# Two transformer blocks on one core: three edits to the order of work in the mixer, and SBUF pools moved to one address rest

## The chip, the cores and the metric

The kernel runs on one core of a Trainium2 chip. Its time is the device time of that core in microseconds (us). Five engines work side by side, each through its own queue in order: PE multiplies matrices, with its weight loads shown apart as PEld; DVE does vector arithmetic; ACT does copies, casts and functions such as exp and sigmoid; POOL helps with a few additions; SP issues the DMA transfers. Instructions wait for each other through semaphores. A transfer brings data from the main memory (DRAM) to SBUF, the on-chip memory, which has 128 partitions; PE writes its sums to PSUM banks, which DVE and ACT read.

## The reference, cut to what matters

The sequence has 512 positions and a width of 1024. The first block has two layers (attention over chunks, then attention through a low-rank latent, each with a convolutional feed-forward part); its result goes to the second block, a feed-forward part, a mixer and another feed-forward part:

```python
x = first_block(x, ...)           # 2 layers: attention + conv FFN each
h = h + 0.5 * gt1 * swiglu(u, w1_gate, w1_up, w1_down)
proj = modulate(rmsnorm(h)) @ w_in          # qa, ka, va, xm, o_pre, ga, gb
ya = diff_attention(qa, ka, va, lam, g_subln)   # 8 heads, p0 - lam * p1, rmsnorm per head
yb = mlstm_branch(xm, o_pre, ...)               # 4 heads of 256 rows, chunkwise mLSTM
merged = sigmoid(ga) * (ya @ w_proj_a) + sigmoid(gb) * (yb @ w_proj_b)
h = h + gt2 * (merged @ w_out)
h = h + 0.5 * gt3 * swiglu(u, w2_gate, w2_up, w2_down)
```

All of it is float32.

## The kernel before, in words

Activations lie transposed, 1024 rows as eight tiles of 128 x 512. A float32 operand is split into two parts of lower precision: the high part by a cast on ACT (`uh`, `yh`, `hidh`, `wh`), the low part as the difference on DVE (`ul`, `hidl`, `wl`). A product of a 128 x 128 weight block and a 128 x 512 tile is then three matmuls (`mm3`, lines 328 to 330: high by high, high by low, low by high). `gemm` runs these over the blocks of one output tile: 24 matmuls for eight blocks. `wload` (L305) fetches a weight row of 1024 columns into one of four `wr` buffers by a DMA on SP's queue and splits it, in one of three `wh` and three `wl` buffers.

Each feed-forward part makes 22 hidden tiles (`hid`, split in two), in groups of eight, eight and six. It multiplies every group by its rows of the down projection. The last three hidden tiles of a part go through `tail` (L431), where `tail_weights` (L421) has split the rest of the weights into four `tw` tiles: the columns are done in two halves of 256, so that the next norm's sum of squares (`colsum`, L365, with `L368` as its matmul) and its normalised tiles of the first half are made while PE works on the second. The output projection of the attentions and of the mixer has the same form, five blocks as full products and three in `tail`.

The mixer (`mix`, L994) does the differential attention (`diff`), then the mLSTM, then the output projection. At the end of the differential attention stand the gate products (`wga`, their sums in the `ps_g` banks, of which there are three) and the projections `wpa` of the attention's result. At L1354 two gate products are written ahead of the loop over the eight output tiles; each turn of the loop takes the sigmoid of the oldest gate sum, makes one `wpa` product, and one further gate product.

`ml_heads` (L1150) runs over the four mLSTM heads. Each makes two tiles `y` (`normed`, L1220). Those of heads 0 to 2 are stored to DRAM (L1245) and fetched again after the heads (L1265), since nothing in SBUF held them; those of head 3 are used in place. `gate` (L1249) makes the gate products `wgb` between the heads' steps. Then come the `wpb` products in groups of three, three and two, the first six blocks of a group ahead of its last two (L1269). Only then does `mix` open the pool `pt`, load the tail weights `woutt` and do the output projection.

The code gives the dependences; the layer that builds the program puts each engine's instructions in an order of its own, so matmuls of several products lie between each other. The order shown below is that of the built programs. Pools are laid out in SBUF by the size of what they hold. The address of a tile within its partition, taken mod 512 bytes ("rest"), is 192 for the split activations `uh`, `ul` and for the split weights `wh`, `wl` in the pool `gp`. The pool `pf` of the first feed-forward part has its hidden tiles `hidh`, `hidl` and its `tw` at rest 192, those of the three later ones have them at rest 128. In the mLSTM's pool `pl` most tiles are at rest 384.

Of the kernel before, what the change touches and what calls it, by code (L numbers as in the profile page):

```python
# [11 lines left out]
F32 = mybir.dt.float32  # L12
F32R = mybir.dt.float32r
I32 = mybir.dt.int32
AF = mybir.ActivationFunctionType
ALU = mybir.AluOpType
PSUM = bass.MemoryType.PSUM

T = 512
P = 128  # L20
# [264 lines left out]
class _K:  # L285
# [186 lines left out]
    def softmax(self, pool, s, n, add, scale, pn):  # L472

        nc = self.nc
        st = self.gp.tile([P, 4], F32, tag="st", bufs=12, name="st")
        p = pool.tile([P, T], F32, tag="p", bufs=pn, name="p")
        nc.vector.tensor_tensor_reduce(p[:, :n], s[:, :n], add, -scale, BIG, ALU.add, ALU.min, accum_out=st[:, 0:1])  # L477
        nc.scalar.activation(p[:, :n], p[:, :n], AF.Exp, bias=st[:, 0:1], scale=-1.0, accum_out=st[:, 1:2])  # L478
        nc.vector.reciprocal(st[:, 2:3], st[:, 1:2])
        return p, st  # L480
# [363 lines left out]
    def rope_tables(self, pr):  # L844
        nc, a = self.nc, self.a

        hpi = pr.tile([P, 1], F32, tag="hpi", name="hpi")
        nc.gpsimd.memset(hpi, math.pi / 2)
        sgn = pr.tile([P, 1], F32, tag="sgn", name="sgn")
        nc.gpsimd.memset(sgn, 1.0)  # L850
        for g in range(4):
            nc.gpsimd.affine_select(sgn[32 * g:32 * g + 32], sgn[32 * g:32 * g + 32], pattern=[[0, 1]],
                                    compare_op=ALU.is_ge, fill=-1.0, base=-16, channel_multiplier=1)
        self.cos = pr.tile([P, T], F32, tag="cos", name="cos")
        self.sin = pr.tile([P, T], F32, tag="sin", name="sin")

        def fill():
            pi32 = self.tmp(dt=I32, tag="acc", bufs=3)
            nc.sync.dma_start(pi32, a["pos"].to_broadcast([P, T]))
            ang = self.tmp(tag="acc", bufs=3)  # L860
            nc.vector.tensor_copy(ang, pi32)
# [12 lines left out]
            nc.scalar.activation(n, ang, AF.Abs)  # L874
            nc.scalar.activation(self.cos, n, AF.Sin, bias=hpi, scale=-1.0)
            nc.scalar.activation(self.sin, ang, AF.Sin)
            nc.vector.tensor_scalar(self.sin, self.sin, sgn, None, ALU.mult)

        return fill
# [114 lines left out]
    def mix(self, norm, ada):  # L994
        nc, a, gp = self.nc, self.a, self.gp
        u = norm.u
        with self.tc.tile_pool(name="px", bufs=1) as px:
            mg = self.diff(u, px)
            self.mlstm(u, mg)
            with self.tc.tile_pool(name="pt", bufs=1) as pt:  # L1000
                tw = self.tail_weights(pt, [("tw", 4)] * 4, "woutt")
                mm = [self.hl(gp, "u", 16, mg[k]) for k in range(8)]
                gt = ada(5)
                for j in range(8):
                    w = self.wload(a["wout"][j], HEAD * P)
                    self.resid(j, self.gemm(w, mm[:HEAD]), gt[:, j:j + 1])
                norm = self.norm_of("g_ff2", ada(7), ada(6))
                self.tail(tw, mm[HEAD:], gt, norm)
        self.dump("hx", self.h)
        return norm  # L1010

    def mlstm(self, u, mg):
        nc, a, gp = self.nc, self.a, self.gp
        dram = {n: [self.dp.tile([P, T], F32, tag=f"{n}{j}", name=f"{n}{j}") for j in range(8)]
                for n in ("mv", "xc", "xs", "so", "sg", "y")}
        for n in ("mq", "mk"):
            dram[n] = [self.dp.tile([4, P, T], F32, tag=f"{n}{h}", name=f"{n}{h}") for h in range(4)]
        with self.tc.tile_pool(name="pl", bufs=1) as pl:
            plc = pl.tile([4, 7 * P], F32, tag="plc", name="plc")
            nc.sync.dma_start(plc, a["pl"])  # L1020
            tri = pl.tile([P, P], F32, tag="tri", name="tri")
            nc.sync.dma_start(tri, a["tri"])
            slr = [pl.tile([P, T], F32, tag="slr", bufs=2, name="slr") for _ in range(2)]
            for q in range(2):
                nc.sync.dma_start(slr[q], a["slr"][q])
            brow = pl.tile([4, T], F32, tag="brow", name="brow")
            self.ml_prep(pl, u, dram, plc, slr, brow)
            self.ml_heads(pl, u, mg, dram, plc, tri, slr, brow)

    def ml_prep(self, pp, u, dram, plc, slr, b):  # L1030
        nc, a = self.nc, self.a
# [2 lines left out]
        nc.gpsimd.memset(wr[:, :960], 0.0)  # L1034
        nc.sync.dma_start(wif32[:, :, 0:8], a["wif"])
        nc.sync.dma_start(wif32[:, :, 32:40], a["wif"])
        wif = pp.tile([P, 24, 40], F32R, tag="wifr", name="wifr")
        nc.scalar.copy(wif, wif32)
        nc.vector.tensor_tensor(wif[:, :, 32:40], wif32[:, :, 32:40], wif[:, :, 0:8].bitcast(F32), ALU.subtract)
        big = lambda: pp.tile([P, T], F32, tag="stg", bufs=5, name="stg")  # L1040
# [109 lines left out]
    def ml_heads(self, pl, u, mg, dram, plc, tri, slr, b):  # L1150
        nc, a, gp = self.nc, self.a, self.gp

        def back(n, j):
            t = pl.tile([P, T], F32, tag="stg", bufs=5, name=n)
            nc.sync.dma_start(t, dram[n][j])
            return t
# [60 lines left out]
                    nc.tensor.matmul(den[:, P * j:], self.onesr, sw[j][q], start=j + q == 0, stop=j + q == 4)  # L1217
            return num, den

        def normed(h, num, den):  # L1220


            em = self.pg()
# [13 lines left out]
            for e in range(2):  # L1237
                j = 2 * h + e
                so, xs = back("so", j), back("xs", j)
                t = self.tmp(tag="tn", bufs=2)  # L1240
                nc.vector.scalar_tensor_tensor(t, num[e], self.col("g_mlnorm", j), r, ALU.mult, ALU.mult)
                nc.vector.tensor_tensor(t, t, so, ALU.mult)
                nc.vector.tensor_tensor(t, t, xs, ALU.add)
                if h < 3:
                    nc.sync.dma_start(dram["y"][j], t)  # L1245
                y.append(t)
            return y
# [4 lines left out]
            nc.scalar.copy(t, self.gemm(w, u))  # L1252
            nc.sync.dma_start(dram["sg"][j], t)

        sw, vt = scores(0), values(0)
        for h in range(4):
            gate(2 * h)
            nxt = scores(h + 1) if h < 3 else None
            gate(2 * h + 1)
            o = output(h, sw, vt)  # L1260
            if h < 3:
                vt = values(h + 1)
            y = normed(h, *o)
            sw = nxt
        ybs = [self.hl(gp, "u", 16, back("y", j)) for j in range(6)] + [self.hl(gp, "u", 16, t) for t in y]  # L1265
        for js in ((0, 1, 2), (3, 4, 5), (6, 7)):
            ws = [self.wload(a["wpb"][j]) for j in js]
            pss = [self.pg() for _ in js]
# [5 lines left out]
            for j, ps in zip(js, pss):  # L1274
                t = back("sg", j)
                nc.scalar.activation(t, t, AF.Sigmoid)
                nc.vector.tensor_tensor(t, ps, t, ALU.mult)
                nc.vector.tensor_tensor(mg[j], mg[j], t, ALU.add)

    def diff(self, u, px):  # L1280
        nc, a, gp = self.nc, self.a, self.gp
# [2 lines left out]
        with self.tc.tile_pool(name="pd", bufs=1) as pd:  # L1284
# [4 lines left out]
            lv = pd.tile([P, 4, 64], F32, tag="lv", name="lv")  # L1289
            for j in range(4):  # L1290
                nc.sync.dma_start(lv[:, j], a["lam"][j:j + 1, :].to_broadcast([P, 64]))
            lc = pd.tile([P, 4], F32, tag="lc", name="lc")
            for j in range(2):
                nc.vector.tensor_tensor_reduce(lv[:, 2 * j], lv[:, 2 * j], lv[:, 2 * j + 1], 1.0, 0.0, ALU.mult,
                                               ALU.add, accum_out=lc[:, j:j + 1])
# [1 line left out]

            nc.vector.tensor_tensor(lc[:, 2:3], lc[:, 1:2], lc[:, 0:1], ALU.subtract)
            nc.vector.tensor_scalar(lc[:, 2:3], lc[:, 2:3], -0.2, None, ALU.add)
            gsub = pd.tile([P, 1], F32, tag="gsub", name="gsub")  # L1300
            nc.vector.tensor_scalar(gsub, self.col("g_subln"), 0.8, None, ALU.mult)
            v32s = {}

# [47 lines left out]
                return probs, v, P, done  # L1351

            self.heads(pd, 8, begin)
            ga = [self.gemm(self.wload(a["wga"][j]), u) for j in range(2)]  # L1354
            slots = [("qk", 10)] * 6 + [("vs", 4)] * 4 + [("p", 4)] * 4 + [("qk", 10)] * 2
            yas = []
            for j, y in enumerate(y32):
                h, l = [pd.tile([P, T], F32R, tag=t, bufs=n, name="yh") for t, n in slots[2 * j:2 * j + 2]]
                self.split(y, h, l)
                yas.append((h, l))  # L1360
            mg = []
            for j in range(8):
                t = self.tmp(tag="acc", bufs=3)
                nc.scalar.activation(t, ga.pop(0), AF.Sigmoid)
                m = px.tile([P, T], F32, tag="mg", bufs=8, name="mg")
                nc.vector.tensor_tensor(m, self.gemm(self.wload(a["wpa"][j]), yas), t, ALU.mult)
                mg.append(m)
                if j < 6:
                    ga.append(self.gemm(self.wload(a["wga"][j + 2]), u))
        return mg  # L1370


# [21 lines left out]
```

## Time and profile before

| | us |
|---|---|
| median of three runs | 2698.45 (2692.15 to 2702.66) |
| the profiled execution | 2697.24 |
| its span, first to last instruction | 2695.5 |
| PE busy | 2587.6 |
| DVE busy | 1756.0 |
| ACT busy | 1204.9 |

The span begins with the first instruction and ends with the last, so the profiled execution has 1.7 us around it. Positions below are us from the span's start. PE is the engine that has work in 96% of the span. A matmul's own duration overlaps the next one's, so for a train of matmuls the distance from one start to the next tells the rate, and the duration does not. The granted clock of PE is given as a share of full speed: 1.00 is 2.4 GHz and 0.50 is 1.2 GHz.

### The profile page before, as it was taken

The page shows a single profiled execution, that of the slowest core. Times are in us where ns is not written, and L with a number is a line of the kernel's source. Part 1 is how long each engine was busy: PE and PEld are TensorE (multiplying, and loading weights), DVE is VectorE, ACT ScalarE, POOL GpSimd, SP SyncE. Part 2 cuts the span into 40 slices and gives each one's busy share as a digit, 9 for nine tenths or more (in the row PEclk, how much of TensorE's full clock was granted, in tenths as well). Part 3 has the DMA queues.
Part 4 walks back from the last instruction along what each step waited for, and adds up shares of the span by engine and source line. Part 5 has one row for each costly group of instructions (what it writes and reads, how often), then busy time and mean ns, then how long its engine had stood idle before and what let it go on. Part 6 is the DMA issues. An engine that isn't in the chain of part 4 may idle for free. (4 is left out here: it accounts for less than half of the span.)

```text
span 2695.5 us, 34803 instructions
## 1 busy us (share of the span) xinstructions
PE 2587.6 (96%) x12666; PEld 2125.6 (79%) x12666; DVE 1756.0 (65%) x3362; ACT 1204.9 (45%) x2118; POOL 90.8 (3%) x138
## 2 busy tenths in 40 slices
PE   8999999999799999999999999999999989999998
PEld 5777888878677887778888888887877767888887
DVE  7887987877788887877633335888365455533344
ACT  5665532335576542324622224667255433522222
POOL 1000200001000100000100001000000000100000
PEclk9999999999899999999999999999999989999999
DMA  8874467672354366664233332442358653233331
GB/s 278 245 212 138 135 208 232 206 240 66 80 147 136 123 209 221 211 228 130 63 97 99 94 110 72 118 114 75 93 185 285 218 170 117 71 97 99 94 113 44
DMA packets 146639, 395.77 MB, mean 147 GB/s; under 512 B 23954, under 2 KB 28178, under 8 KB 146468
## 3 DMA queue, kind: packets, MB, share of 16 engines
q1 hardware_dynamic: 146468, 393.55, 47.0%
q8 instruction: 100, 1.64, 0.3%
q14 instruction: 71, 0.58, 0.1%
HBM read 341.05 MB, written 26.21 MB: 136 GB/s over the span
## 5 line engine op out<-in xcount | busy, mean ns | idle before, releaser
L328 PE MATMUL ps_g<-uh,wh 128*128 128x512 f32 (+1 forms) x2028 | 779.6, 388 | 23.5 <-ACT uh L341 11.6
L329 PE MATMUL ps_g<-ul,wh 128*128 128x512 f32 (+1 forms) x2028 | 785.1, 388 | 16.0 <-POOL ul L401 13.7
L330 PE MATMUL ps_g<-uh,wl 128*128 128x512 f32 (+1 forms) x2028 | 778.5, 385 | 0.0
L311 ACT CAST wh<-wr 128x1024 fp32r<-128x1024 f32 (+3 forms) x398 | 396.9, 998 | 821.6 <-PE ps_g L329 568.2
L312 DVE TENSOR_TENSOR wl<-wr,wh 128x1024 fp32r<-128x1024 f32 (+3 forms) x398 | 462.2, 1162 | 255.9 <-ACT wh L311 246.5
L328 PEld LDWEIGHTS ps_g<-uh,wh 128*128 128x128 f32 x2028 | 382.1, 190 | 111.4 <-ACT uh L341 14.3
L329 PEld LDWEIGHTS ps_g<-ul,wh 128*128 128x128 f32 x2028 | 384.5, 190 | 95.7 <-POOL ul L401 20.0
L330 PEld LDWEIGHTS ps_g<-uh,wl 128*128 128x128 f32 x2028 | 384.1, 190 | 74.8 <-issue 2.0
L462 DVE CUSTOM_DVE_ANT_0 wr<-wr,cact 128x1024 f32<-128x1024 f32 x184 | 226.8, 1235 | 111.8 <-DMA wr<-mod 110.8
L328 PE MATMUL ps_g<-hidh,wh 128*128 128x512 f32 x608 | 239.0, 393 | 0.9 <-ACT wh L311 0.8
L330 PE MATMUL ps_g<-hidh,wl 128*128 128x512 f32 x608 | 238.8, 393 | 0.0
L329 PE MATMUL ps_g<-hidl,wh 128*128 128x512 f32 x608 | 238.8, 393 | 0.0
L328 PEld LDWEIGHTS ps_g<-hidh,wh 128*128 128x128 f32 x608 | 113.8, 187 | 28.6 <-ACT wh L311 1.2
L330 PEld LDWEIGHTS ps_g<-hidh,wl 128*128 128x128 f32 x608 | 113.8, 187 | 27.0
L329 PEld LDWEIGHTS ps_g<-hidl,wh 128*128 128x128 f32 x608 | 113.8, 187 | 26.9
L445 DVE SCALAR_TENSOR_TENSOR h<-ps_g,hg,h 128x512 f32<-128x512 f32 (+1 forms) x64 | 43.7, 683 | 125.8 <-PE ps_g L330 125.7
L478 ACT ACTIVATE p<-p,st 128x128 f32<-128x128 f32 (+1 forms) x192 | 107.2, 559 | 41.2 <-DVE st L477 40.1
L341 ACT CAST hidh<-cv 128x512 fp32r<-128x512 f32 x88 | 54.7, 621 | 137.4 <-DVE cv L799 129.9
L986 DVE TENSOR_TENSOR cv<-ps_g,cv 128x512 f32<-128x512 f32 x38 | 26.3, 692 | 121.2 <-PE ps_g L330 119.8
L362 POOL TENSOR_TENSOR acc<-acc,sq 128x256 f32<-128x256 f32 x42 | 32.8, 782 | 2002.5 <-ACT sq L361 1107.5
L445 DVE SCALAR_TENSOR_TENSOR h<-ps_g,mods,h 128x512 f32<-128x512 f32 (+1 forms) x112 | 72.8, 652 | 38.5 <-PE ps_g L330 38.3
L398 ACT ACTIVATE uh<-tn,mods 128x256 fp32r<-128x256 f32 (+1 forms) x120 | 60.5, 519 | 62.4 <-DVE tn L394 61.6
(379 smaller groups left out, 4189.7 us busy)
## 6 DMA issues: line engine op xcount, KB each, us to landing
wr<-mod SPq DMA_DIRECT2D x184, 512.0 KB, 4.3
wr<-fin SPq DMA_DIRECT2D x88, 512.0 KB, 4.3
wr<-fout SPq DMA_DIRECT2D x32, 512.0 KB, 3.4
wr<-w1g SPq DMA_DIRECT2D x22, 512.0 KB, 3.6
wr<-w1u SPq DMA_DIRECT2D x22, 512.0 KB, 3.6
wr<-w2g SPq DMA_DIRECT2D x22, 512.0 KB, 3.6
wr<-w2u SPq DMA_DIRECT2D x22, 512.0 KB, 3.6
wr<-wqk SPq DMA_DIRECT2D x16, 512.0 KB, 5.0
```

What stands on the lines that cost most here:

```text
L311: nc.scalar.copy(h[:, :n], r[:, :n])
L312: nc.vector.tensor_tensor(l[:, :n], r[:, :n], h[:, :n].bitcast(F32), ALU.subtract)
L328: mm(ps, wh, xh, start=start, stop=False)
L329: mm(ps, wh, xl, start=False, stop=False)
L330: mm(ps, wl, xh, start=False, stop=stop)
L341: self.nc.scalar.copy(h, src)
L362: (eng or nc.vector).tensor_tensor(acc[:, cs], acc[:, cs], s[:, cs], ALU.add)
L398: nc.scalar.activation(h[:, cs], t, AF.Identity, bias=sh)
L445: self.nc.vector.scalar_tensor_tensor(self.h[j][:, cs], ps, g, self.h[j][:, cs], ALU.mult, ALU.add)
L462: nc.vector.tensor_tensor_reduce(w, w, cact, 1.0, 0.0, ALU.mult, ALU.add, accum_out=self.mods[:, j:j + 1])
L478: nc.scalar.activation(p[:, :n], p[:, :n], AF.Exp, bias=st[:, 0:1], scale=-1.0, accum_out=st[:, 1:2])
L986: nc.vector.tensor_tensor(t, pss[1], t, ALU.mult)
```

## The change

No computation is added or removed. There are three parts.

**Addresses.** Four small tiles (`hpi`, `sgn`, `lc`, `gsub`) leave the pools in which they were and take buffers of the tag `st` in `gp`, which has 14 of these in place of 12; `wifr` becomes 4096 bytes where it had 3840. With these sizes the pools opened behind `gp` begin 64 bytes later, and what follows `wifr` in `pl` begins 320 bytes later: the hidden tiles of the three later feed-forward parts go from rest 128 to 192, the tiles of the first attention (its `tw` among them) and the `tw` of the output projection from 128 to 192, and most of those of `pl` from 384 to 192.

**Differential attention.** Three gate products are written ahead instead of two, and the sigmoid of a gate sum is taken one turn earlier.

**mLSTM and output projection.** `y` of heads 0 and 1 is still stored, but fetched already during head 3, into a tile `first` that takes a free buffer of the scores; `y` of head 2 is written straight into another, `four`, and makes no trip. The split of the six tiles and of the tail weights `woutt`, which take four buffers of the same tag, is written ahead of the `wpb` products, and `out` runs the output projection within the same pool.

```diff
-        st = self.gp.tile([P, 4], F32, tag="st", bufs=12, name="st")
+        st = self.gp.tile([P, 4], F32, tag="st", bufs=14, name="st")
...
-        wif = pp.tile([P, 24, 40], F32R, tag="wifr", name="wifr")
+        wif = pp.tile([P, 1024], F32R, tag="wifr", name="wifr")[:, :960].rearrange("p (k c) -> p k c", c=40)
...
+            four = pl.tile([P, 4, T], F32, tag="xs", bufs=4, name="y") if h == 2 else None
+            y += normed(h, *o, to=four)
+            if h == 2:
+                first = pl.tile([P, 4, T], F32, tag="xs", bufs=4, name="y")
+                for j in range(4):
+                    nc.sync.dma_start(first[:, j], dram["y"][j])
+                y = [first[:, j] for j in range(4)] + y[-2:]
             sw = nxt
-        ybs = [self.hl(gp, "u", 16, back("y", j)) for j in range(6)] + [self.hl(gp, "u", 16, t) for t in y]
+        ybs = [self.hl(gp, "u", 16, t) for t in y]
+        tw = self.tail_weights(pl, [("xs", 4)] * 4, "woutt")
...
-            ga = [self.gemm(self.wload(a["wga"][j]), u) for j in range(2)]
+            ga = [self.gemm(self.wload(a["wga"][j]), u) for j in range(3)]
+            sig = []
+
+            def sigmoid():
+                sig.append(self.tmp(tag="acc", bufs=3))
+                nc.scalar.activation(sig[-1], ga.pop(0), AF.Sigmoid)
...
+            sigmoid()
             for j in range(8):
-                t = self.tmp(tag="acc", bufs=3)
-                nc.scalar.activation(t, ga.pop(0), AF.Sigmoid)
+                if ga:
+                    sigmoid()
                 m = px.tile([P, T], F32, tag="mg", bufs=8, name="mg")
-                nc.vector.tensor_tensor(m, self.gemm(self.wload(a["wpa"][j]), yas), t, ALU.mult)
+                nc.vector.tensor_tensor(m, self.gemm(self.wload(a["wpa"][j]), yas), sig.pop(0), ALU.mult)
                 mg.append(m)
-                if j < 6:
-                    ga.append(self.gemm(self.wload(a["wga"][j + 2]), u))
+                if j < 5:
+                    ga.append(self.gemm(self.wload(a["wga"][j + 3]), u))
```

On PE, at the end of the differential attention, this stood around the last head's transposes (`ps_t`) and its output (`ps_o`); `ps_g<-yh` is the first `wpa` product, which needs the heads' results:

```order
L328 MATMUL ps_g_17277<-yh_17244,wh_17273 128x512
L515 MATMUL ps_t_17136<-ident_65,p_17093 128x128 x3
L329 MATMUL ps_g_17277<-yh_17245,wh_17273 128x512
L330 MATMUL ps_g_17277<-yh_17244,wl_17274 128x512
L328 MATMUL ps_g_17277<-yh_17248,wh_17273 128x512
L515 MATMUL ps_t_17142<-ident_65,p_17116 128x128 x4
L328 MATMUL ps_o_17149<-pth_17011,vsh_16788 128x512
```

The same place now has the third gate product (`ps_g_17242<-uh`, 24 matmuls), whose operands have long been there:

```order
L330 MATMUL ps_g_17242<-uh_14579,wl_17239 128x512
L515 MATMUL ps_t_17142<-ident_65,p_17116 128x128 x4
L328 MATMUL ps_g_17242<-uh_14581,wh_17238 128x512
L329 MATMUL ps_g_17242<-ul_14582,wh_17238 128x512
L330 MATMUL ps_g_17242<-uh_14581,wl_17239 128x512
L328 MATMUL ps_g_17242<-uh_14583,wh_17238 128x512
L329 MATMUL ps_g_17242<-ul_14584,wh_17238 128x512
L330 MATMUL ps_g_17242<-uh_14583,wl_17239 128x512
L328 MATMUL ps_o_17149<-pth_17011,vsh_16788 128x512
```

The `wpa` products have moved behind the last head's output.

On SP's queue of before, the end of the heads reads so: the store of the last `y` of head 2, a load of `wpb` weights, the reloads of head 3's operands (`so`, `xs`), the store of the last gate (`sg_17774`), and the first two of the six fetches of `y`, with the seventh `wpb` load between them:

```order
L1245 DMA y_17780<-tn 128x512
L308 DMA wr<-wpb 128x1024
L1155 DMA so<-so_17765 128x512
L1253 DMA sg_17774<-sg 128x512
L1155 DMA xs<-xs_17757 128x512
L1155 DMA so<-so_17766 128x512
L1155 DMA xs<-xs_17758 128x512
L1155 DMA y<-y_17775 128x512
L308 DMA wr<-wpb 128x1024
L1155 DMA y<-y_17776 128x512
```

And now, where the four fetches of `y` stand earlier and the loads of `woutt` earlier still:

```order
L1269 DMA y<-y_17779 128x512
L1254 DMA sg_17773<-sg 128x512
L1156 DMA so<-so_17765 128x512
L1254 DMA sg_17774<-sg 128x512
L1156 DMA xs<-xs_17757 128x512
L1156 DMA so<-so_17766 128x512
L1156 DMA xs<-xs_17758 128x512
L308 DMA wr<-wpb 128x1024 x3
L1156 DMA sg<-sg_17767 128x512
L308 DMA wr<-wpb 128x1024 x4
```

All eight `wpb` loads have moved behind the stores of the last gates `sg_17773` and `sg_17774`; before, six of them stood ahead of the last gate's store. The `woutt` loads have moved from behind the `wpb` loads to before the fetches of `y`.

On PE, where the `wpb` products end (`ps_g_20135`), before went on with parts of the tail in two other banks, `ps_s` and `ps_t`:

```order
L330 MATMUL ps_g_20135<-uh_19902,wl_20131 128x512
L328 MATMUL ps_s_20469<-uh_20238,tw_20198 128x256
L329 MATMUL ps_s_20469<-ul_20239,tw_20198 128x256
L328 MATMUL ps_t_20497<-uh_20238,tw_20198 128x256
L329 MATMUL ps_t_20497<-ul_20239,tw_20198 128x256
L330 MATMUL ps_s_20469<-uh_20238,tw_20199 128x256
```

Now it goes on with the full products of the output projection (`wh_20238` is its first weight):

```order
L330 MATMUL ps_g_20145<-uh_19892,wl_20141 128x512
L328 MATMUL ps_g_20242<-uh_20204,wh_20238 128x512
L329 MATMUL ps_g_20242<-ul_20205,wh_20238 128x512
L330 MATMUL ps_g_20242<-uh_20204,wl_20239 128x512
L328 MATMUL ps_g_20242<-uh_20208,wh_20238 128x512
```

The tail's matmuls have moved behind all eight of these.

## Rows read from the trace of the kernel before

**Rows 1.** The page's first part: busy time, share of the span, instructions.

```profile
PE 2587.6 (96%) x12666; PEld 2125.6 (79%) x12666; DVE 1756.0 (65%) x3362; ACT 1204.9 (45%) x2118; POOL 90.8 (3%) x138
```

**Rows 2.** Stages: length, PE busy (matmuls), granted clock, DMA share, GB/s.

```profile
1010.00:1035.00 25.00, 25.00 (x109) 1.00 0.59 194
...
2205.30:2219.00 13.70, 9.03 (x18) 0.50 0.34 113
2259.56:2311.39 51.83, 47.23 (x269) 0.97 0.41 122
```

**Rows 3.** Tile hidh, one stage each: count, duration ns, first and last start.

```profile
L328 PE MATMUL ps_g<-hidh,wh x64: 389/389/389, 388.3 to 431.1; 128*128 128x512 f32 x64
...
L328 PE MATMUL ps_g<-hidh,wh x64: 394/394/394, 1008.9 to 1053.0; 128*128 128x512 f32 x64
...
L328 PE MATMUL ps_g<-hidh,wh x64: 394/394/394, 2415.9 to 2460.0; 128*128 128x512 f32 x64
```

**Rows 4.** Groups of PE by line and form: count, busy, mean ns, idle before.

```profile
L328 PE MATMUL ps_g<-uh,wh 128*128 128x512 f32 x1868 | 738.2, 396 | 23.5 <-ACT uh L341 11.6 <-DVE mods L463 4.6 <-DVE cv L796 2.6
...
L328 PE MATMUL ps_g<-hidh,wh 128*128 128x512 f32 x608 | 239.0, 393 | 0.9 <-ACT wh L311 0.8
...
L328 PE MATMUL ps_g<-xs,wh 128*128 128x512 f32 x48 | 19.1, 397 | 0.5 <-ACT wh L311 0.5
```

**Rows 5.** Tile tw, half-width products of the first and second attention's projection.

```profile
L329 PE MATMUL ps_g<-ul,tw x24: 278/280/467, 263.0 to 281.5; 128*128 128x256 f32 x24
...
L329 PE MATMUL ps_g<-ul,tw x24: 278/283/306, 883.6 to 902.9; 128*128 128x256 f32 x24
```

**Rows 6.** Timeline of PE, end of differential attention: start, duration, [idle before, releaser].

```profile
1871.52 0.50 PE L328 MATMUL ps_g<-yh,wh 128*128 128x512 f32 x1 [1.96 <-ACT yh L341]
1873.33 0.63 PE L515 MATMUL ps_t<-ident,p 128*128 128x128 f32 x4 [1.32 <-DVE p L1340]
...
1879.17 0.51 PE L328 MATMUL ps_g<-yh,wh 128*128 128x512 f32 x1 [0.60 <-ACT yh L341]
```

**Rows 7.** Timeline of ACT at the same place.

```profile
1879.50 0.60 ACT L1346 ACTIVATE acc<-ps_o 128x512 f32<-128x512 f32 x1
1880.12 1.28 ACT L1364 ACT_TABLE_LOAD   x1
1881.42 0.60 ACT L1364 ACTIVATE acc<-ps_g 128x512 f32<-128x512 f32 x1
```

**Rows 8.** Timeline of PE, from the last mLSTM head to the end of wpb.

```profile
2202.50 1.12 PE L1224 MATMUL ps_g<-brow,plc 4*128 4x512 f32 x2
2207.40 0.80 PE L328 MATMUL ps_g<-uh,wh 128*128 128x512 f32 x1 [3.78 <-ACT uh L341]
...
2214.12 0.80 PE L329 MATMUL ps_g<-ul,wh 128*128 128x512 f32 x1 [1.48 <-DVE ul L342]
...
2259.33 0.39 PE L330 MATMUL ps_g<-uh,wl 128*128 128x512 f32 x1
```

**Rows 9.** Timeline of ACT at the end of the heads.

```profile
2198.48 1.05 ACT L311 CAST wh<-wr 128x1024 fp32r<-128x1024 f32 x1 [5.44 <-PE ps_g L329]
2199.43 0.58 ACT L1252 COPY sg<-ps_g 128x512 f32<-128x512 f32 x1
...
2206.73 0.62 ACT L341 CAST uh<-y 128x512 fp32r<-128x512 f32 x1 [2.38 <-DMA y<-y]
```

**Rows 10.** Timeline of DVE at the end of the heads.

```profile
2205.11 1.42 DVE L362 TENSOR_TENSOR acc<-acc,sq 128x512 f32<-128x512 f32 x2
```

**Rows 11.** DMA issues: count, KB each, median us from issue to landing.

```profile
wr<-wpb SPq DMA_DIRECT2D x8, 512.0 KB, 4.5
```

**Rows 12.** Timeline of PE and ACT in the output projection.

```profile
2262.85 0.36 PE L328 MATMUL ps_s<-uh,tw 128*128 128x256 f32 x1 [3.14 <-issue]
...
2302.65 0.70 PE L368 MATMUL ps_s<-acc,onesr 128*128 128x256 f32 x2 [1.25 <-POOL acc L362]
...
2261.92 3.03 ACT L311 CAST tw<-wr 128x768 fp32r<-128x768 f32 x4 [1.40 <-DVE mg L1278]
```

More of the change, by code (lines that the diff above doesn't have):

```diff
@@ L845, in rope_tables @@
         nc, a = self.nc, self.a
-        hpi = pr.tile([P, 1], F32, tag="hpi", name="hpi")
+        hpi, sgn = [self.gp.tile([P, 4], F32, tag="st", bufs=14, name="small")[:, 0:1] for _ in range(2)]
         nc.gpsimd.memset(hpi, math.pi / 2)
-        sgn = pr.tile([P, 1], F32, tag="sgn", name="sgn")
         nc.gpsimd.memset(sgn, 1.0)
@@ L997, in mix, with out @@
         with self.tc.tile_pool(name="px", bufs=1) as px:
[L998 to L1001, printed above, removed]
+            def out(tw):
                 mm = [self.hl(gp, "u", 16, mg[k]) for k in range(8)]
@@ L1008, in mix, with mlstm @@
                 self.tail(tw, mm[HEAD:], gt, norm)
+                return norm
+            mg = self.diff(u, px)
+            norm = self.mlstm(u, mg, out)
         self.dump("hx", self.h)
         return norm
-    def mlstm(self, u, mg):
+    def mlstm(self, u, mg, out):
         nc, a, gp = self.nc, self.a, self.gp
@@ L1027, in mlstm @@
             self.ml_prep(pl, u, dram, plc, slr, brow)
-            self.ml_heads(pl, u, mg, dram, plc, tri, slr, brow)
+            return out(self.ml_heads(pl, u, mg, dram, plc, tri, slr, brow))
     def ml_prep(self, pp, u, dram, plc, slr, b):
@@ L1218, in output, with normed @@
             return num, den
-        def normed(h, num, den):
+        def normed(h, num, den, to=None):
             em = self.pg()
@@ L1239, in normed @@
                 so, xs = back("so", j), back("xs", j)
-                t = self.tmp(tag="tn", bufs=2)
+                t = to[:, e] if to is not None else self.tmp(tag="tn", bufs=2)
                 nc.vector.scalar_tensor_tensor(t, num[e], self.col("g_mlnorm", j), r, ALU.mult, ALU.mult)
@@ L1243, in normed @@
                 nc.vector.tensor_tensor(t, t, xs, ALU.add)
-                if h < 3:
+                if h < 2:
                     nc.sync.dma_start(dram["y"][j], t)
@@ L1253, in gate @@
             nc.sync.dma_start(dram["sg"][j], t)
-        sw, vt = scores(0), values(0)
+        sw, vt, y = scores(0), values(0), []
         for h in range(4):
@@ L1262, in ml_heads @@
                 vt = values(h + 1)
-            y = normed(h, *o)
+            four = pl.tile([P, 4, T], F32, tag="xs", bufs=4, name="y") if h == 2 else None
[5 more added lines that the diff above has]
+                y = [first[:, j] for j in range(4)] + y[-2:]
             sw = nxt
-        ybs = [self.hl(gp, "u", 16, back("y", j)) for j in range(6)] + [self.hl(gp, "u", 16, t) for t in y]
+        ybs = [self.hl(gp, "u", 16, t) for t in y]
+        tw = self.tail_weights(pl, [("xs", 4)] * 4, "woutt")
         for js in ((0, 1, 2), (3, 4, 5), (6, 7)):
@@ L1278, in ml_heads @@
                 nc.vector.tensor_tensor(mg[j], mg[j], t, ALU.add)
+        return tw
     def diff(self, u, px):
@@ L1291, in diff @@
                 nc.sync.dma_start(lv[:, j], a["lam"][j:j + 1, :].to_broadcast([P, 64]))
-            lc = pd.tile([P, 4], F32, tag="lc", name="lc")
+            lc = gp.tile([P, 4], F32, tag="st", bufs=14, name="lc")
             for j in range(2):
@@ L1299, in diff @@
             nc.vector.tensor_scalar(lc[:, 2:3], lc[:, 2:3], -0.2, None, ALU.add)
-            gsub = pd.tile([P, 1], F32, tag="gsub", name="gsub")
+            gsub = gp.tile([P, 4], F32, tag="st", bufs=14, name="gsub")[:, 0:1]
             nc.vector.tensor_scalar(gsub, self.col("g_subln"), 0.8, None, ALU.mult)
```

## The prediction

> **What bounds the kernel now.** I read the page's first part first. PE is busy for 2587.6 us, 96% of the span, and no other engine passes 65% [rows 1], so PE sets the end: an edit counts only if it closes a gap of PE, raises its clock or brings the starts of its matmuls closer together. I then cut the span by stages. In the third feed-forward stage shown, PE is busy for all of 25.00 us at full clock [rows 2]; gaps have nothing to give there, and the distance between starts is all that is left. So I read the tile view of the hidden tiles and compared the stages. Last I read the timelines around the three places in the mixer where PE stands still or runs at half clock.
>
> **Addresses.** The same 64 triples of matmuls, in the down projection of a feed-forward part, take from first to last start 431.1 - 388.3 = 42.8 us in the first part and 44.1 us in the second (1053.0 - 1008.9) and the fourth (2460.0 - 2415.9) [rows 3]. From the first start of the first triple to that of the last there are 3 x 63 = 189 intervals: 226.5 ns against 233.3 ns. First and second part run the same code. What differs is the address: in the first part hidden tiles and weights both lie at rest 192, in the others the hidden tiles lie at 128. Durations say the same, 389 against 394 ns. The change puts the three later parts at the rest that the first one has. There are 608 x 3 = 1824 such full-width matmuls [rows 4], a quarter of them in the first part, so 1368 gain 6.8 ns each: 9.3 us. The 48 x 3 = 144 matmuls on `xs` [rows 4] have a mean of 397 ns, like the slow kind, and go from rest 384 to 192; at the same step they give 1.0 us. Against this stand half-width matmuls of split activations and `tw`: where activations and `tw` share rest 192 (second attention) the median is 283 ns, where `tw` lies at 128 (first attention) 280 ns [rows 5]. Such a tail has 16 products of nine matmuls, 144. Two tails move from the shorter kind to the longer, 288 matmuls; so do the half-width products at the starts of the three later feed-forward parts, two products in two halves of eight triples in each part, 288 more: 576 x 3 ns = 1.7 us lost. The sum is -8.6 us. The bounds are 0, if the addresses aren't the cause, and -10.3, if the half-width loss does not come. I take -8.6, since rows 3 show both kinds for one code.
>
> Rows 3 are where the notes speak against the change. The Trainium skill, page "TensorE: Matmul & The Clock Gate", section "Step-by-step: what each phase is for", says that PE has two independent read ports, so loading the next weights does not take bandwidth from the running matmul. By that rule the place of the weights against the activations would not matter and this part would be worth nothing; the trace does not agree, as 226.5 and 233.3 ns stand for one code.
>
> **End of the differential attention.** PE stands still for 1.96 us for the cast of a head's result, 1.32 us for the last probabilities and 0.60 us for the last head's cast [rows 6], 3.9 us together. The third gate product puts 24 matmuls, 24 x 0.2265 = 5.4 us of work that waits for none of these, in that place. What is late next: the norm's column sum now stands right behind the last head's output, and ACT must first do the square, 0.60 us, with a copy as long ahead of it; the first `wpa` product behind it needs a `ps_g` bank, all three of which hold gate sums until the first sigmoid, which is an ACT table load of 1.28 us and 0.60 us of sigmoid after the square [rows 7]. That is 1.2 + 1.9 = 3.1 us of new wait at worst, less what the square's wait covers of the table load. Behind the waiting column sum the whole of PE's queue waits. From -3.9 + 3.1 I get -0.8; at best, with the table loaded under the column sum's own time, the new wait is 1.2 and the part gives -2.7. At worst the last probabilities (1.32) stay as well and the part costs +0.5. I take -1.3, nearer to the first, since the table load stands behind the square on one queue.
>
> **End of the mLSTM.** PE ends the small matmul of the last head at 2202.50 + 1.12 = 2203.62. It then waits until 2207.40 for a cast of `y` [rows 8], which waited for the fetch of `y` [rows 9], and through two further waits until 2214.12, from where it goes on without a stop to 2259.33 [rows 8]. Between 2203.62 and 2214.12 lie four matmuls and a column sum, some 1.8 us of work, so 8.7 us are lost. From 2205.30 to 2219.00 the granted clock is 0.50, the 1.2 GHz level [rows 2]; behind 2214.12 that stretches 4.9 us of matmuls, which at the full clock would be half as long: 2.4 us more. Together 11.1 us.
>
> With the change four `y` tiles have been fetched during head 3 and two were never stored, so their casts are done before PE is free. What is late next are the `wpb` weights: the loads now stand behind the last gate's store, whose copy ends at 2199.43 + 0.58 = 2200.0 [rows 9]. Landing takes 4.5 us [rows 11] and the cast 1.05 [rows 9]; with some 1 us for issue and handing over, the first product starts at 2206.6. The column sum of the last head is ready near then, since DVE's sum ends at 2205.11 + 1.42 = 2206.5 [rows 10]. So PE waits about 3.0 us there, and I allow 0.6 for the low half of the weights behind their cast. Its clock will fall for a while after such a wait, as it did here; I put 1.2 us, half of the loss now. Left are 4.8 of 11.1 us: -6.3. The later `wpb` loads have 5.4 us of PE's work each to come in, and two of the four buffers are then always ahead. At best the weights are there when PE comes, -9; at worst each is late as the first is, which is priced below. I take -6.3.
>
> **Output projection.** From the last matmul of `wpb` until the tail's last one PE needs 51.83 us [rows 2]. Its work is 8 x 15 full matmuls, 120 x 0.2265 = 27.2 us, 144 half-width ones, 17.0 us at 0.118 (an estimate between half of 0.2265 and the 18.5 / 142 = 0.130 us that the first attention's tail needs with its waits [rows 5]; their new rest is counted above), and two column sums, 0.7 us: 44.9. So 6.9 us are lost, 3.14 of them as the tail weights were still being cast (ACT 2261.92 to 2264.95) and 1.25 before the column sum [rows 12], the rest at half clock. Now the tail weights are split during head 3, and the full products need five of the merged tiles, which are ready by then; the first tail product comes 27 us later. No wait is left in front. I keep 0.7 us for the column sums, whose chain over DVE, ACT and POOL has the same work, and get -6.2. Were the first output weights late by a landing (4.5), -1.7 would remain; that is the upper bound, and -6.9 the lower.
>
> **Sum.** -8.6 - 1.3 - 6.3 - 6.2 = -22.4 us. The profiled execution, 2697.24 us, is 1.2 below the median of the runs, 2698.45. I set the change against its own execution, 2674.8, and put the forecast 1.2 higher, at the median: 2676. By the bounds of the parts it lies between -28.9 (-10.3 - 2.7 - 9 - 6.9) and -1.2.
>
> **The rivals.** (1) The rests aren't the cause of 233 ns. For it: the first part also comes first, with other weights and other transfers beside it. Against it: `xs`, which is in another stage and at a third rest, has the slow duration too. Then the first part gives 0 and the time is 2684.6. (2) The late `wpb` weights cost as much as `y` did: all eight loads stand behind one store, and every product of the first groups waits for its own landing. Against it: four buffers are free at once. The mLSTM's part gives 0, 2682. (3) Slower than before: sharing one rest costs, at the moved tiles. The half-width products are slower where rests agree [rows 5], and all but the full-width matmuls on `uh` and `wh` (1868 x 3 = 5604) and the 1824 hidden ones [rows 4] could be of that kind, 12666 [rows 1] - 7428 = 5238 matmuls at 3 ns, 15.7 us lost. With no gain in the feed-forward parts and the mLSTM's and the projection's gains halved (-6.3), the sum is +8.1 with the differential attention at -1.3: 2706.5. It decides from the point where the loss per matmul passes 1.5 ns, as 6.3 + 1.3 = 7.6 us are gained against it over 5238 matmuls. Against it: of the matmuls that move, most are half or less as wide, and PE waits for others beside them. (4) No part shows, as the scheduler puts the waits elsewhere: 2696.
>
> **How the numbers follow.** The forecast has 0.70 (2668 to 2681), the first rival 0.11, the second 0.10, the third 0.03, the fourth 0.06. What a measurement of this kernel can tell from no change is about 0.5%, 13.5 us: under 2685.0 counts as faster. The forecast, the second rival and half of the first make 0.85 faster; the rest of the first, the fourth and most of the third make 0.13 the same; 0.02, where the third costs more than 3 ns, is slower. The range of 8 in 10 reaches down to 2667, near the lower bound of the sum with a little left out, and up over both likely rivals to 2689.
>
> **What would show it.** In the profile after, the 64 triples of the second and fourth part should take 42.8 us and 389 ns. At the end of the heads one wait of some 3 us on the cast of the `wpb` weights should stand, none on `y`. The stretch from the last `wpb` matmul to the tail's end should fall to about 45.5 us. At the differential attention the waits on `yh` and `p` should go, and one in front of the column sum and the first `wpa` product come. The forecast is wrong if the triples still take 44.1 us, if every `wpb` product waits, or if a new wait of several us comes behind the output projection, where the chain of the next norm is unchanged.

## The result and the profile after

The changed kernel takes 2679.15 us, median of four runs, against 2699.2 us for the kernel before on the same chip; the ratio is 0.9932, 95% interval 0.9914 to 0.9949, which is 18.4 us. Timed again (run `after_again`, below) the ratio is 0.9921, 0.9908 to 0.9933: 21.3 us of 2690.65. The forecast was 22.4 us less, 2676.

The two profiled executions differ by 15 us only (2682.12 against 2697.24), and not all of that difference comes from the change. I compared the start of the same matmul in both traces. Up to the first hidden product the changed kernel had lost 8.8 us, 2 of them at the first norm and most of the others in the first attention, where PE waits for keys on their way through DRAM. These are the waits of PE after (total us, times, longest); before, the two totals were 3.9 and 1.0 us:

```profile
PE ps_s L555 <- DMA k<-k: 6.1, 5, 2.9
...
PE ps_s L556 <- DMA k<-k: 4.0, 5, 1.4
```

That stretch took 388.3 us in the profile of before and 397.1 after, and between 388.8 and 395.2 in the twelve profiles below: 391.7 to 392.2 in the three with the old addresses, 388.8 to 395.2 in those with new ones. Two executions of one program on one chip, `best2` and `best2_again`, took 389.2 and 395.2 us. So each place below is read by its own length, and not by the difference of the spans.

The page's first part, after; PE is busy for 19.3 us less, and the busy time of the other engines has hardly changed:

```profile
PE 2568.3 (96%) x12666; PEld 2122.5 (79%) x12666; DVE 1755.1 (65%) x3362; ACT 1206.5 (45%) x2118; POOL 91.5 (3%) x138
```

The tile view of the hidden tiles, second and fourth feed-forward part [rows 3]: 42.8 us from first to last start in both (the starts below are rounded), and 389 ns, as the first part had before.

```profile
L328 PE MATMUL ps_g<-hidh,wh x64: 389/389/389, 1017.8 to 1060.7; 128*128 128x512 f32 x64
...
L328 PE MATMUL ps_g<-hidh,wh x64: 389/389/389, 2403.7 to 2446.5; 128*128 128x512 f32 x64
```

The tails that moved to rest 192 have the longer duration, 283 ns [rows 5]; here those of the first attention and of the output projection:

```profile
L329 PE MATMUL ps_g<-ul,tw x24: 278/283/472, 271.9 to 290.9; 128*128 128x256 f32 x24
...
L329 PE MATMUL ps_g<-ul,tw x24: 281/283/283, 2280.4 to 2298.5; 128*128 128x256 f32 x24
```

PE's timeline at the end of the differential attention [rows 6], and ACT's under it [rows 7]. The waits on `yh` and `p` are gone; the column sum waits for its square, then the first `wpa` product for the sigmoid that empties its bank:

```profile
1874.03 0.50 PE L329 MATMUL ps_o<-ptl,vsh 128*128 128x512 f32 x1 [0.44 <-DVE ptl L342]
...
1877.51 1.12 PE L368 MATMUL ps_o<-acc,onesr 128*128 128x512 f32 x2 [1.58 <-ACT acc L1355]
1879.41 0.50 PE L328 MATMUL ps_g<-yh,wh 128*128 128x512 f32 x1 [0.78 <-ACT acc L1368]
```

```profile
1876.85 0.60 ACT L1355 ACTIVATE acc<-ps_o 128x512 f32<-128x512 f32 x1
1877.47 1.28 ACT L1368 ACT_TABLE_LOAD   x1
1878.77 0.60 ACT L1368 ACTIVATE acc<-ps_g 128x512 f32<-128x512 f32 x1
```

PE at the end of the mLSTM [rows 8]. The wait on `y` is gone. In its place stand the forecast one on the weights, 3.98 us, and one that was not forecast, 1.77 us, of the second `wpb` product on a DVE operation of the last head:

```profile
2199.23 1.12 PE L1225 MATMUL ps_g<-brow,plc 4*128 4x512 f32 x2
2204.34 0.80 PE L328 MATMUL ps_g<-uh,wh 128*128 128x512 f32 x1 [3.98 <-ACT wh L311]
...
2213.17 0.47 PE L328 MATMUL ps_g<-uh,wh 128*128 128x512 f32 x1 [1.77 <-DVE tn L1242]
...
2253.10 0.39 PE L328 MATMUL ps_g<-uh,wh 128*128 128x512 f32 x1
```

SP's queue, and ACT and DVE at that place: the loads are issued from 2197.57, ACT casts the first at 2203.24 when it has landed, and DVE reads the head's numerator (`ps_g`) at 2212.27:

```profile
2197.10 0.37 SPq L1156 DMA_DIRECT2D xs<-xs  x1
2197.57 3.16 SPq L308 DMA_DIRECT2D wr<-wpb  x3
```

```profile
2203.24 1.04 ACT L311 CAST wh<-wr 128x1024 fp32r<-128x1024 f32 x1 [2.16 <-DMA wr<-wpb]
...
2212.27 1.41 DVE L1242 SCALAR_TENSOR_TENSOR tn<-ps_g,par,rr 128x512 f32<-128x512 f32 x2
```

Stages of PE after (length, busy, matmuls, granted clock, DMA share, GB/s): the output projection, 45.73 us where it was 51.83 [rows 2], with PE busy throughout at full clock, and the half clock behind the new wait, 6.8 us where it was 13.7 [rows 2]:

```profile
2253.00:2298.73 45.73, 45.69 (x270) 1.00 0.35 103
...
2201.30:2208.10 6.80, 3.77 (x7) 0.50 0.97 355
```

### The profile page after: what moved, and what is told of

It reads as the page before. It is cut to its first block, busy times and chain, and to the rows that moved or that the text cites. A ratio compares the mean times of both kernels' runs of the same rounds, so it can differ in the third digit from the quotient of the medians.

```text
span 2680.3 us, 34798 instructions
## 1 busy us (share of the span) xinstructions
PE 2568.3 (96%) x12666; PEld 2122.5 (79%) x12666; DVE 1755.1 (65%) x3362; ACT 1206.5 (45%) x2118; POOL 91.5 (3%) x138
## 4 chain that ended last, share of the span: by engine, by line
PE 44%; DMA 2%; DVE 2%; ACT 1%; issue 1%; POOL 0%; SPq 0%; DVEq 0%; POOLq 0%; ACTq 0%
PE ps_g L328 12%; PE ps_g L329 12%; PE ps_g L330 12%; PE ps_t L329 1%; PE ps_t L328 1%; PE ps_t L330 1%; DMA stg<-xc 1%; POOL ul L401 0%; PE ps_o L368 0%; PE ps_s L555 0%; PE ps_s L556 0%; PE ps_s L328 0%; DMA mv<-mv 0%; PE ps_s L330 0%; PE ps_s L329 0%
## 5 line engine op out<-in xcount | busy, mean ns | idle before, releaser
L478 ACT ACTIVATE p<-p,st 128x128 f32<-128x128 f32 (+1 forms) x192 | 107.4, 560 | 44.1 <-DVE st L477 43.1
```

## The experiments

Verdicts rest on the length of a place in each trace and, where a kernel was run several times, on the ratio to the kernel before on the same chip. Lengths go from the start of one matmul to the start of another; a part's tail, or a product, ends here with the start of its last matmul.

**The parts, one by one.** `addr_only` is the kernel before with the first part of the change, `order_only` the changed kernel without it:

```diff
-        st = self.gp.tile([P, 4], F32, tag="st", bufs=12, name="st")
+        st = self.gp.tile([P, 4], F32, tag="st", bufs=14, name="st")
...
-        wif = pp.tile([P, 24, 40], F32R, tag="wifr", name="wifr")
+        wif = pp.tile([P, 1024], F32R, tag="wifr", name="wifr")[:, :960].rearrange("p (k c) -> p k c", c=40)
```

> The kernel before with the addresses alone changed. Theory (the common rest closes up the matmuls): the 64 triples of the three later feed-forward parts take 42.8 us instead of 44.1, about 9 us in all, and the time is 2690 +- 2. Rival (the rest is not the cause): 44.1 us as before and 2698. Second rival (the new addresses make the first attention wait longer for its reloaded keys, which the profile of the changed kernel shows as 8.8 us lost before 300 us): 42.8 us, but the first hid product starts near 397 us instead of 388, and the time is 2698 as well.

> The changed kernel with the addresses of before. Theory: the three feed-forward parts take 44.1 us per 64 triples, the mixer keeps its gains (about 4.8 us at the end of the differential attention, 3.6 at the end of the mLSTM, 5.8 in the output projection), 2685 +- 2. Rival (addresses cost in the first attention): the first hid product starts near 388 us. If the 8.8 us are chance, it may stand anywhere from 386 to 398.

`addr_only`: ratio 0.9967 (0.9953 to 0.9980), 8.9 us. `order_only`: 0.9956 (0.9939 to 0.9973), 11.8 us. The fourth part's triples in the one and in the other:

```profile
L328 PE MATMUL ps_g<-hidh,wh x64: 389/389/389, 2397.7 to 2440.6; 128*128 128x512 f32 x64
```

```profile
L328 PE MATMUL ps_g<-hidh,wh x64: 394/394/394, 2394.1 to 2438.2; 128*128 128x512 f32 x64
```

The third part, from its first hidden product to its tail's end, takes 263.11 us in the one and 266.19 in the other, and within 0.02 us so in every other run with the same rests; the fourth part does the same: 3.08 us each. The first hidden product starts at 392.8 and 392.0 us, so the addresses are not what made the stretch before it 8.8 us longer; whether they cost a us or two there stays open.

`diff_only` is the kernel before with the second part of the change, `mlstm_only` with the third:

> The kernel before with the three gate products ahead alone. Theory: from the last matmuls of the heads to the first product of the mLSTM 4.8 us less than before, 2694. Rival (the forecast's own size): 1.3 us less, 2698.

> The kernel before with the part on the mLSTM's outputs and the tail weights alone, at the addresses of before. Theory: a wait of about 4 us on the wpb weights and one of 1.8 us of the second wpb product on its PSUM bank; end of the mLSTM 3.6 us less and output projection 5.8 us less than before, 2689.5. Rival (the forecast: only the first wait): 12.5 us less, 2686.5.

`diff_only`: ratio 0.9971 (0.9956 to 0.9986), `mlstm_only`: 0.9973 (0.9960 to 0.9985); these are 7.8 and 7.3 us, with intervals 7 to 8 us wide, so the places decide. The stretch read for the second part of the change runs from the third feed-forward part's end to the last `wpa` product. Before, it takes 294.0 us, with 3.4 us at half clock in it. With the edit it takes 290.8 us where as much is at half clock (`diff_only`), 292.2 where 6.8 us are (`order_only`; without the edit 294.9 and 295.1 in `addr_only` and `mlstm_only`), 289.2 to 289.7 where none is. The half clock of before, of `diff_only` and of `order_only` (length, PE busy, matmuls, granted clock, DMA share, GB/s):

```profile
1874.20:1877.60 3.40, 2.97 (x8) 0.50 0.00 0
```

```profile
1870.70:1874.10 3.40, 3.40 (x9) 0.50 0.47 151
```

```profile
1872.90:1879.70 6.80, 6.05 (x14) 0.50 0.33 106
```

With as much half clock on both sides that is 2.7 to 3.2 us, and 4.3 to 4.8 against 294.0 when the clock holds. The theory's 4.8 is right only where the clock holds; the rival's 1.3 is too small. PE's waits in `diff_only` are those of the changed kernel:

```profile
1865.03 0.50 PE L329 MATMUL ps_o<-ptl,vsh 128*128 128x512 f32 x1 [0.47 <-DVE ptl L342]
1868.52 1.12 PE L368 MATMUL ps_o<-acc,onesr 128*128 128x512 f32 x2 [1.58 <-ACT acc L1346]
1870.42 0.58 PE L328 MATMUL ps_g<-yh,wh 128*128 128x512 f32 x1 [0.78 <-ACT acc L1359]
```

And in `mlstm_only` both waits at the end of the mLSTM are there:

```profile
2198.70 0.79 PE L328 MATMUL ps_g<-uh,wh 128*128 128x512 f32 x1 [4.64 <-ACT wh L311]
2207.53 0.47 PE L328 MATMUL ps_g<-uh,wh 128*128 128x512 f32 x1 [1.69 <-DVE tn L1243]
```

From the last pair of small matmuls of the heads to the output projection: 57.1 us before, 54.5 (`mlstm_only`), 53.4 (`order_only`), 53.9 and 53.6 (the changed kernel, twice), 53.3 in `rests_a` and `rests_b`, which have the same order. (The output projection of before is taken to begin where the `wpb` products end, so that its wait of 3.14 us [rows 12] belongs to it.) From there to the tail's last start: 51.7 before, 45.2 at the old rests, 45.5 at the new. In `mlstm_only` both stretches together gain 9.0 us (2.5 and 6.5): the theory's 9.4 fits, the rival's 12.5 does not.

**Which rest it is.** A spacer ahead of each feed-forward part's pool moves its hidden tiles (words of four bytes; here those of `rests_a`):

```diff
+        self.nf = getattr(self, "nf", -1) + 1
-        with self.tc.tile_pool(name="pf", bufs=1) as pf:
+        with self.tc.tile_pool(name="pad", bufs=1) as pd, self.tc.tile_pool(name="pf", bufs=1) as pf:
+            self.nc.gpsimd.memset(pd.tile([P, (16, 96, 80, 32)[self.nf]], F32, tag="pad", name="pad")[:, 0:1], 0.0)
```

> The changed kernel with a small spacer ahead of each feed-forward part's pool, so that the hidden tiles lie at rest 256, 64, 0 and 320 in the four parts (weights at 192 as ever). Theory (both operands must share one rest mod 512): 64 triples take 44.1 us and 389 turns to 394 ns in all four parts. Rival (only rests that are like 192 mod 128, that is 64, 192, 320, 448, are fast): 42.8 us in the second and fourth part, 44.1 in the first and third. Second rival (only rest 128 and its like are slow): 42.8 us everywhere.

> The same with rests 448, 32, 160 and 224. Theory: 44.1 us in all four parts. Rival (like 192 mod 128): 42.8 us in the first part, 44.1 in the other three. Second rival: 42.8 us everywhere.

Rests 256, 64, 0 and 320, in this order:

```profile
L328 PE MATMUL ps_g<-hidh,wh x64: 394/394/398, 388.8 to 432.0; 128*128 128x512 f32 x64
...
L328 PE MATMUL ps_g<-hidh,wh x64: 392/394/398, 1006.0 to 1050.0; 128*128 128x512 f32 x64
...
L328 PE MATMUL ps_g<-hidh,wh x64: 394/394/397, 1384.7 to 1427.9; 128*128 128x512 f32 x64
...
L328 PE MATMUL ps_g<-hidh,wh x64: 392/394/398, 2384.5 to 2428.6; 128*128 128x512 f32 x64
```

Rests 448, 32, 160 and 224:

```profile
L328 PE MATMUL ps_g<-hidh,wh x64: 389/389/389, 391.3 to 434.1; 128*128 128x512 f32 x64
...
L328 PE MATMUL ps_g<-hidh,wh x64: 392/392/398, 1010.1 to 1054.2; 128*128 128x512 f32 x64
...
L328 PE MATMUL ps_g<-hidh,wh x64: 395/396/397, 1392.4 to 1436.5; 128*128 128x512 f32 x64
...
L328 PE MATMUL ps_g<-hidh,wh x64: 393/396/399, 2402.8 to 2446.9; 128*128 128x512 f32 x64
```

All three theories fail. 448 is as fast as 192 (42.8 us), 0 and 256 lie between (43.2 to 43.3), the other five are slow (44.0 to 44.1): with the weights at 192, 448 goes like 192, 0 like 256 and 64 like 320, so the rate repeats every 256 bytes, not 512. To tell whether the distance or the activations' own rest counts, `w256` has 64 bytes between the two in `gp`:

```diff
+            self.spacer = self.gp.tile([P, 16], F32, tag="spacer", name="spacer")
         h, l = dst or (self.gp.tile([P, 1024], F32R, tag="wh", bufs=3, name="wh"),
```

> The changed kernel with a spacer of 64 bytes in gp between the activations and the weights: uh and ul stay at rest 192, the weights wh and wl and the pools behind them, with the hidden tiles, go to 256. Theory A (what counts is the distance between the two operands mod 256): hidden tiles and weights lie together as before, 64 triples in 42.8 us, but the 5604 full-width matmuls on uh go from 389 to 394 ns and lose 6.8 ns each, 38 us, so 2705 or more. Theory B (what counts is the rest of the activations alone, 192 or 448 the best): the matmuls on uh stay at 389 ns and the hidden ones, at 256, take 43.3 us as in the first part at 256; 2680.

The hidden tiles, at 256 with their weights, keep 42.8 us; the matmuls on `uh`, at 192 as ever, go to 394 ns (here those in the `ps_t` banks, before and in `w256`):

```profile
L331 PE MATMUL ps_g<-hidh,wh x64: 389/389/398, 1012.8 to 1055.6; 128*128 128x512 f32 x64
```

```profile
L328 PE MATMUL ps_t<-uh,wh 128*128 128x512 f32 x192 | 74.8, 389 | 0.0
```

```profile
L331 PE MATMUL ps_t<-uh,wh 128*128 128x512 f32 x192 | 75.7, 394 | 0.0
```

Their starts say the same. Twelve matmuls apart they lie 2.72 us from each other in the changed kernel, 226.7 ns each, and 2.80 us in `w256`, 233.3 ns each:

```profile
1075.64 0.39 PE L328 MATMUL ps_g<-uh,wh 128*128 128x512 f32 x1
...
1078.36 0.39 PE L328 MATMUL ps_g<-uh,wh 128*128 128x512 f32 x1
```

```profile
1080.11 0.39 PE L331 MATMUL ps_g<-uh,wh 128*128 128x512 f32 x1
...
1082.91 0.39 PE L331 MATMUL ps_g<-uh,wh 128*128 128x512 f32 x1
```

That is theory A. The one run took 2693.71 us, 6.3 above the kernel before on that chip and so some 27 above the changed one at its ratio of 0.992, not 38: part of the loss seems to lie under other waits, which no run shows.

**The two new waits.** `banks` gives the three sums of a group one bank of each kind; `best1` has this, the third gate product in a bank of `ps_s`, and the first `wpb` load ahead of the tail weights; `best2` has the two bank edits alone, shown here:

```diff
-            ga = [self.gemm(self.wload(a["wga"][j]), u) for j in range(3)]
+            ga = [self.gemm(self.wload(a["wga"][j]), u, tag="ggs"[j]) for j in range(3)]
...
-            pss = [self.pg() for _ in js]
+            pss = [self.pg(tag=t) for t in "gst"[:len(js)]]
```

> The changed kernel with the sums of the wpb products in one bank each of ps_g, ps_s and ps_t instead of three of ps_g. Theory (the second product waited for the bank that still held the last head's numerator): the wait of 1.8 us on DVE's tn goes, the wait of 4 us on the wpb weights stays, 1.8 us less between the last small matmul of the heads and the end of the output projection. Rival (the second product would wait at the same place for its weights, which come late too): the wait stays with ACT's or DVE's split of the weights as its releaser, less than 0.5 us gained.

> The changed kernel with the banks as in the run before, the first wpb load ahead of the tail weights, and the third gate product of the differential attention in a bank of ps_s. Theory: at the end of the mLSTM neither the weights nor the bank are waited for, and some 5 us go there; at the end of the differential attention the first wpa product no longer waits for a sigmoid, 0.8 us more; 2673 where the changed kernel has 2679 (ratio to before 0.991). Rival (the column sum's input, which is ready 3 us after PE is free, holds PE anyway): 2 to 3 us only.

> The changed kernel with the two bank edits alone (third gate product in ps_s; wpb sums in ps_g, ps_s and ps_t), the wpb loads where the change has them. Theory: 3.4 us less than the changed kernel at the end of the differential attention, as in the run with all three edits, and 0.9 us less at the end of the mLSTM, as in the run with the banks alone; ratio to before 0.991. Rival (the early load is worth its waits after all): the ratio is above that of the run with all three edits, 0.9907.

PE's only wait over 0.1 us between the heads and the output projection in `banks`, and the two of `best1` behind the last small matmul:

```profile
2192.97 0.79 PE L328 MATMUL ps_g<-uh,wh 128*128 128x512 f32 x1 [4.42 <-ACT wh L311]
```

```profile
2207.44 0.50 PE L328 MATMUL ps_g<-uh,wh 128*128 128x512 f32 x1 [1.96 <-ACT uh L341]
2215.63 0.50 PE L330 MATMUL ps_g<-uh,wl 128*128 128x512 f32 x1 [0.52 <-DVE wl L312]
```

So the second wait was the bank: it goes, and the stretch takes 52.5 us (52.0 and 52.7 in `best2`, run twice) where runs of the changed order have 53.3 to 53.9. `best1` shows the first wait was the weights' place in the queue: it goes as well, but PE is then held by the last head's own `y` and by another split, and the stretch is 53.3 us, no gain, nearer its rival than its theory. Its differential attention takes 286.2 us, 3.0 to 3.5 less than the changed kernel without half clock, where the theory had 0.8: not the wait on the sigmoid alone goes but all three waits, 0.44, 1.58 and 0.78 us. With a bank free, the first `wpa` product starts ahead of the column sum and fills PE's time until the sum's input is there, as in `best2_again`:

```profile
1865.83 0.39 PE L328 MATMUL ps_g<-yh,wh 128*128 128x512 f32 x1
...
1870.12 1.13 PE L368 MATMUL ps_o<-acc,onesr 128*128 128x512 f32 x2
```

So `best1` came out at the ratio of its theory by luck: the gain it has lies in the other of its two places. Ratios: `best1` 0.9907 (0.9890 to 0.9924), `best2` 0.9900 (0.9884 to 0.9917); whether the early load is worth anything, these two do not tell apart. Then the changed kernel and the one with the two bank edits on one chip:

> The changed kernel once more, beside the one with the two bank edits on the same chip. Theory (the gains of the change sit in five places of the trace, the rest of the difference between two profiles is chance): ratio to before 0.992 to 0.993; from the third part's first hidden start to the tail's end 263.1 us, from the heads' last small matmul to the output projection's end 99 us, and less than 397 us to the first hidden start. Rival (the address part makes the first attention slower): again some 397 us.

> The changed kernel with the two bank edits once more. Theory: 0.16% to 0.2% faster than the changed kernel on the same chip (4.3 us), ratio to before 0.990 to 0.991. Rival (its earlier ratio was a lucky chip): the same as the changed kernel.

The changed kernel takes 2668.3 us (0.9921, 0.9908 to 0.9933), the one with the two bank edits 2662.02 (0.9896, 0.9881 to 0.9911): the second is 6 us faster than the first in the medians, but the intervals overlap a little, so that its rival is unlikely but not excluded. The changed kernel's places are as forecast, 263.1 and 99.1 us. Its first hidden product starts at 394.3 us, at 395.2 in the other, so the rival of some 397 does not hold.

## Why the prediction was right, point by point

**Addresses: right, -8.6 forecast.** The third part and the fourth each gain 3.08 us. The second has the same matmuls and the same shorter triples, and its whole is blurred by other waits (375 to 385 us from its first hidden product to the third part's), so I count 3.08 there too. The `xs` stage gives 0.5 (76.6 to 76.1 us), and the output projection's tail takes 0.3 back: -9.4, and -8.9 timed alone, with an interval of 5 to 13. The half-width products lose 2 ns each and not 3, as their starts go from 118 to 120 ns apart; of the 1.7 us that they were to lose only these 0.3 show in the length of a stretch, and at the other places no loss stands out from the differences between runs. The cause was named a common rest, and a rest is taken mod 512; the runs say distance mod 256. The first rival, by which the rests are not the cause, is out. The Trainium skill's rule of two independent read ports (page "TensorE: Matmul & The Clock Gate", section "Step-by-step: what each phase is for") would have left the pace unmoved by the weights' place. This case's traces do not agree: in `w256`, in which only that place moved for `uh`, 226.7 ns turn to 233.3.

**End of the differential attention: mechanism right, size off.** The step that failed is "3.9 us together": I left out two shorter waits on `yh` and one on the last casts, 1.14 us in the same stretch, and the half clock behind them:

```profile
1868.82 0.50 PE L329 MATMUL ps_g<-yh,wh 128*128 128x512 f32 x1 [0.25 <-DVE yh L342]
...
1874.63 0.80 PE L328 MATMUL ps_o<-pth,vsh 128*128 128x512 f32 x1 [0.67 <-ACT pth L341]
...
1879.90 0.50 PE L329 MATMUL ps_g<-yh,wh 128*128 128x512 f32 x1 [0.22 <-DVE yh L342]
```

The new waits were priced 3.1 at worst and are 0.44 + 1.58 + 0.78 = 2.8. Measured is -2.7 to -3.2 with as much half clock on both sides, and -4.3 to -4.8 where the clock held; I had -1.3.

**End of the mLSTM: half of it.** Forecast -6.3; from the last small matmul to the output projection it is -2.5 to -3.7. The wait on the weights came as said, 3.3 to 4.6 us in the runs of this order instead of 3.0 + 0.6. The step that failed is that "the later `wpb` loads have 5.4 us of PE's work each to come in" was all that was asked of the second product, and the sum has no term for its PSUM bank: all three `ps_g` banks were held by the last head, two of them until DVE reads the numerators behind the column sum's chain, a wait of 1.0 to 1.8 us. `banks` removes that wait and wins 0.8 to 1.4 us. In the profile after, 3.2 of the 6.3 us came: the bank took 1.77 of the missing 3.1 and the weights 0.4 more than priced; the rest, some 0.9, lies behind these waits, at half clock in part, and no run takes it apart.

**Output projection: right.** Forecast -6.2 without the new rest, which is counted above; at the old rests 51.7 became 45.2 us, -6.5.

The measured terms come to -9.4 - 3 - 3.3 - 6.5 = -22.2 us, and the timings to -18.4 and -21.3. That the sum of the forecast fits so well is partly luck: the end of the differential attention was forecast some 2 us too small and the end of the mLSTM 3 us too large.

## What to carry to other kernels

Where PE is busy all the time, compare the distance between starts of the same matmul in two stages: here 3% of a stage's pace, 0.3% of the time, hid in the tiles' addresses, where no wait shows it. When a wait is taken away, look up for the next two products, not for one, which bank each needs and who reads it last: both new waits that PE has on a bank went when a product got a bank of another kind. A difference of two profiles is read place by place, since the stretch that waits for DRAM differed by 6 us between two executions of one program.

## What was not expected of the hardware

With moving tiles of 128 x 512 the pace was 226.5 ns where tile and weights lay at one rest mod 256, about 229 where the tile lay 64 above, and 233 where it lay 32, 96, 128, 192 or 224 above; half-width ones go the other way, 120 ns apart (283 ns long) at one rest and 118 (280 long) where the tile lies 64 above. Why is open. So is what decides on the half clock: the same stretch of the differential attention had 0, 3.4 or 6.8 us of it in runs of the same order there, with nearly the same waits of PE, and each 3.4 us cost 0.9 to 1.5. It had some in all three profiles without the edit and in three of the eight with it alone, so the edit may help the clock hold; that is not shown.
